# Products with w_o between the last heads of both mixers, and weight splits taken from POOL

## Chip, cores and metric

One core of one Trainium2 chip. The metric is device time of one execution in microseconds (us), the median of the runs shown.

## What is computed

The reference, cut to what matters here (x is 512 x 1024, two layers, all in fp32):

```python
for i in range(DEPTH):                      # 0: mixer A, 1: mixer B
    h = rms_norm(x, g_mix_pre[i])
    proj = h @ w_in[i]                      # q: 12 heads of 64, k and v: 3 heads, qm: 4 heads
    ...
    tok = mixer_a(...) if kind == 0 else mixer_b(...)
    mo = memory_attention(qm, km, vm)       # 4 heads on 256 memory rows
    o = jnp.concatenate([tok, mo], axis=-1) @ w_o[i]
    x = x + rms_norm(o, g_mix_post[i])
    h = rms_norm(x, g_ffn_pre[i])
    gu = h @ w_gate_up[i]
    f = (jax.nn.silu(gu[..., :D_FF]) * gu[..., D_FF:]) @ w_down[i]
    x = x + rms_norm(f, g_ffn_post[i])
```

Mixer A attends to a band of 128 tokens to either side with a sink logit per head; mixer B attends to all 512 tokens, with norms on q and k.

## The kernel before

Every fp32 operand of a large product is split into two parts, a high one (`hi`) and the rest (`lo`). A product is then three matmuls (`mm3`, lines 220 to 222 in the trace). `split` makes the parts: `hi` by ACT (line 230) or, if bit 2 of its last argument is set, by POOL (line 228); `lo` by DVE (line 234) or, with bit 1, by POOL (line 232). `unit` fetches a piece of a weight matrix of 128 x 1024 (or 768) by a DMA on SP's queue into one of three buffers and splits it, in halves of 512 columns where it is placed among the heads; four pairs of split units exist at a time.

The token rows lie in four row tiles of 128 (t = 0 to 3). A mixer runs in one order for PE that the kernel writes out: pieces of work are put at a place x, counted in heads, with `put(x, f)`, sorted and then issued. The places come from the table `PACE`, one entry per mixer, as do the engines for splits (`kw` for w_kv, `mw` for the memory weights, `qw` for w_q, `owm` for w_o, `tw` for the heads' outputs). The order of the other engines is made by a scheduler that follows the dependences.

At a mixer's start come the transposes of the normed rows (hT), the products with w_kv (`kv_pieces`), w_q (`q_pieces`) and the memory weights (`mem_pieces`). Then 12 token heads and 4 memory heads: scores (lines 511 and 512, memory scores 545 and 546), exponentials on ACT (528, 550), normalising of p on POOL (566), transposes of p on PE (576), splits of them (`th`, `tl`), the value product (590, 591) and the sum into `tok` on DVE (599).

`heads_out` places the work on w_o among the last heads: four units of the first 512 output columns, the splits of `tok` into `th` (`part(k)`, k = 0 to 7, one for each pair of heads), and the products of k = 0 to 5 for the row tiles 0 and 1, six matmuls at a time. `mix_out` follows the heads: it finishes the first 512 columns, squares them (ACT) and multiplies them by the gain (DVE), then does the second 512 columns row tile by row tile, with a norm and the residual. `ffn_out` is the end of the feed-forward part; for each row tile `join` adds, squares and multiplies, `post_norm` adds the residual and gives the normed row h for the next layer.

PSUM's eight banks are called acc (2), s (3), pv (1) and t (2). Scores take s, value products pv, transposes of p and of the rows t, transposes of q for c > 0 acc. `bank` hands acc, acc, s, s, s, pv out in turn for the products with w_o.

```python
for k in range(KD):
    put(xs[k], lambda k=k: part(k))
for k in range(NH // 2):
    put(max(x0 + k * dx, xs[k] + 0.001), lambda k=k: prod(k))
```

Of the kernel before, what the change touches and what calls it, by code (L numbers as in the profile page):

```python
# [15 lines left out]
P = 128  # L16
# [15 lines left out]
BIG = 1e37  # L32
LOTS = ((0, 8), (8, 14), (14, 22))

PACE = [{'lag': 1.692, 'vlag': 0.479, 'jstep': 0.213, 'kstep': 0.375, 'klag': 0.742, 'qoff': [0.212, 0.126, 0.099], 'qlag': 1.02, 'late': 0.252, 'moff': -0.235, 'mdur': 0.562, 'mlag': 0.697, 'kw': [1, 0, 2, 0], 'mw': [2, 1, 1, 0], 'qw': [1, 0, 0, 1, 3, 3, 3, 3], 'hoff': 1.262, 'ow': 10.288, 'ox': 14.385, 'od': 0.906, 'hstep': 0.872, 'hlag': 1.742, 'hjstep': 0.135, 'hvlag': 0.751, 'owm': [3, 3, 3, 3, 3, 2, 0, 1], 'q0step': 0.27, 'q0off': -0.032, 'q0lag': 0.919, 'm0off': -0.078, 'm0dur': 0.002, 'm0lead': 1.887, 'mlead': 1.201, 'qlead': 0.921, 'q0lead': 1.555, 'qstep': 1.002, 'tw': [0, 0, 0, 1, 0, 1, 0, 0], 'h2off': 0}, {'lag': 1.824, 'vlag': 0.535, 'jstep': 0.218, 'kstep': 0.777, 'klag': 1.715, 'qoff': [-0.027, -0.162, -0.027], 'qlag': 1.189, 'late': 2.15, 'moff': -0.088, 'mdur': 0.384, 'mlag': 1.205, 'kw': [0, 0, 0, 0], 'mw': [2, 2, 0, 3], 'qw': [1, 0, 0, 0, 0, 3, 1, 1], 'hoff': 0, 'ow': 12.899, 'ox': 15.498, 'od': 0.513, 'hstep': 0.946, 'hlag': 1.847, 'hjstep': 0.295, 'hvlag': 0.568, 'owm': [3, 3, 3, 0, 3, 2, 0, 3], 'q0step': 0.718, 'q0off': -0.018, 'q0lag': 1.136, 'm0off': -1.059, 'm0dur': 0.171, 'm0lead': 2.465, 'mlead': 3.162, 'qlead': 1.895, 'q0lead': 1.42, 'qstep': 0.998, 'tw': [0, 1, 2, 3, 1, 0, 1, 0], 'h2off': 0.016}]
# [137 lines left out]
class Trunk:  # L173
# [139 lines left out]
    def bank(self):  # L313

        tag, bufs = (("acc", 2), ("acc", 2), ("s", 3), ("s", 3), ("s", 3), ("pv", 1))[self.nbank % 6]
        self.nbank += 1
        return self.ps.tile([P, 512], F32, tag=tag, name="ps", bufs=bufs)
# [15 lines left out]
    def mem_pieces(self, l, mk, put, x0, dx, lag, xw):  # L333

        w, ps = {}, []
        for u in range(4):
            self.unit(self.a["wm"][l, u], self.side(l, "mw", u), put=put, x=xw[u], dst=w, key=u)

        def prod(u, m):
            if u == 0:  # L340
                ps.append(self.ps.tile([P, 512], F32, tag="s", name="ps", bufs=3))
# [71 lines left out]
    def kv_pieces(self, l):  # L413
# [4 lines left out]
        w = self.wkv if l == 0 else [self.unit(self.a["wkv"][l, u], side=self.side(l, "kw", u)) for u in range(4)]  # L418
# [32 lines left out]
    def q_pieces(self, l, c, qTs, put, x0, lead):  # L451
# [29 lines left out]
        def stage(t, st):  # L481
            if c:
# [15 lines left out]
    def score(self, hd, i):  # L498
# [10 lines left out]
        s = self.ps.tile([P, 512], F32, tag="s", name="s", bufs=3)  # L509
# [23 lines left out]
    def score_mem(self, hd, i):  # L533
# [8 lines left out]
        s = self.ps.tile([P, 2, NMEM], F32, tag="s", name="s", bufs=3)  # L542
# [185 lines left out]
    def heads_out(self, l, put, xw, xs, x0, dx):  # L728
# [3 lines left out]
        for u in range(4):  # L732
            self.unit(self.a["wo"][l, 0, u], self.side(l, "owm", u), put=put, x=xw + u / 4, dst=self.wo, key=u)
# [8 lines left out]
        def prod(k):  # L742
            if k == 0:
                self.po.extend(self.bank() for _ in range(2))
            for t in range(2):
                self.prod(self.po[t], self.heads, KD, k, t, self.wo[k // 2])

        for k in range(KD):
            put(xs[k], lambda k=k: part(k))
        for k in range(NH // 2):  # L750
            put(max(x0 + k * dx, xs[k] + 0.001), lambda k=k: prod(k))
# [4 lines left out]
    def mix_out(self, l, forms, resid, dst):  # L756
# [57 lines left out]
    def tagged(self, tag):  # L814
        return self.ps.tile([P, 512], F32, tag=tag, name="ps", bufs={"acc": 2, "s": 3, "pv": 1, "t": 2}[tag])

    def ffn_out(self, get, w, fs, o, head, gpost, gpre, resid, dst, rs):
# [26 lines left out]
        for t in range(NT):  # L844
# [237 lines left out]
    def run(self):  # L1082
        tc, nc, a = self.tc, self.nc, self.a
        with ExitStack() as top:
# [5 lines left out]
            self.ps, self.nbank = self.psum(top, "ps"), 0  # L1090
# [84 lines left out]
```

## Time and profile before

| | us |
|---|---|
| median of 3 runs (1162.67 to 1164.7) | 1163.73 |
| profiled execution | 1161.5 |
| its span on the core | 1159.7 |
| PE busy | 1106.9 |
| DVE busy | 840.9 |
| ACT busy | 644.7 |
| POOL busy | 264.6 |

Times within the trace count from the start of the span. Mixer A's heads end near 183, mixer B's start lies at 570 to 640 and its heads end near 767; the feed-forward parts lie behind each mixer. A row of a timeline gives start, busy time, engine, line, operation and tiles, and in brackets how long the engine stood idle before it and what released it. Matmuls are pipelined: a row's own time is longer than the step from one matmul to the next.

### The profile page before, as it was taken

The page shows a single profiled execution, that of the slowest core. Times are in us where ns is not written, and L with a number is a line of the kernel's source. Part 1 is how long each engine was busy: PE and PEld are TensorE (multiplying, and loading weights), DVE is VectorE, ACT ScalarE, POOL GpSimd, SP SyncE. Part 2 cuts the span into 40 slices and gives each one's busy share as a digit, 9 for nine tenths or more (in the row PEclk, how much of TensorE's full clock was granted, in tenths as well). Part 3 has the DMA queues.
Part 4 walks back from the last instruction along what each step waited for, and adds up shares of the span by engine and source line. Part 5 has one row for each costly group of instructions (what it writes and reads, how often), then busy time and mean ns, then how long its engine had stood idle before and what let it go on. Part 6 is the DMA issues. An engine that isn't in the chain of part 4 may idle for free.

```text
span 1159.7 us, 19436 instructions
## 1 busy us (share of the span) xinstructions
PE 1106.9 (95%) x7448; PEld 1016.6 (88%) x7448; DVE 840.9 (73%) x1432; ACT 644.7 (56%) x1308; POOL 264.6 (23%) x394
## 2 busy tenths in 40 slices
PE   5999989999999999999898999799999999999997
PEld 4989878899989989998788888577999899899985
DVE  5678884798637866885778998846997458658854
ACT  5568783665425534653436888845665246436531
POOL 6445573200000000000454764433000000000001
PEclk9999999999999999999999999999999999999999
DMA  7521124533422342225523110234234323413243
GB/s 269 189 74 37 37 74 134 189 114 109 154 65 73 110 145 73 97 87 191 174 93 106 37 37 2 69 116 150 68 115 140 107 73 110 142 41 110 92 163 109
DMA packets 34316, 124.06 MB, mean 107 GB/s; under 512 B 3872, under 2 KB 4000, under 8 KB 34096
## 3 DMA queue, kind: packets, MB, share of 16 engines
q1 hardware_dynamic: 33984, 122.24, 32.0%
q8 instruction: 58, 0.95, 0.3%
q0 software_dynamic: 240, 0.60, 0.2%
q14 instruction: 34, 0.28, 0.1%
HBM read 112.33 MB, written 10.49 MB: 106 GB/s over the span
## 4 chain that ended last, share of the span: by engine, by line
PE 78%; DVE 9%; ACT 5%; POOL 3%; issue 3%; DMA 1%; SPq 0%; POOLq 0%; DVEq 0%; ACTq 0%
PE ps L220 12%; PE ps L221 12%; PE ps L222 12%; PE ps L930 11%; PE ps L932 11%; PE ps L931 11%; PE tp L576 2%; PE o L591 1%; PE o L590 1%; PE s L511 1%; DVE tl L234 1%; PE s L512 1%; DMA raw<-in_wkv_dram 1%; ACT whi L230 1%; ACT p L528 1%
## 5 line engine op out<-in xcount | busy, mean ns | idle before, releaser
L230 ACT ACTIVATE whi<-raw 128x1024 fp32r<-128x1024 f32 (+2 forms) x177 | 150.6, 860 | 208.6 <-PE ps L222 104.2
L234 DVE TENSOR_TENSOR wlo<-raw,whi 128x1024 fp32r<-128x1024 f32 (+2 forms) x171 | 171.5, 1009 | 89.9 <-ACT whi L230 74.2
L930 PE MATMUL ps<-sf,whi 128*128 128x256 f32 x640 | 180.3, 282 | 0.1
L932 PE MATMUL ps<-sf,whi 128*128 128x256 f32 x640 | 180.2, 282 | 0.0
L931 PE MATMUL ps<-sf,wlo 128*128 128x256 f32 x640 | 179.8, 281 | 0.0
L254 POOL TENSOR_SCALAR e<-sso 128x1 f32<-128x1 f32 x8 | 3.4, 423 | 634.7 <-ACT junk L249 634.6
L220 PE MATMUL ps<-whi,f 128*128 128x512 f32 x352 | 137.3, 390 | 0.0
L222 PE MATMUL ps<-whi,f 128*128 128x512 f32 x352 | 137.0, 389 | 0.0
L221 PE MATMUL ps<-wlo,f 128*128 128x512 f32 x352 | 137.0, 389 | 0.0
L930 PE MATMUL ps<-a,whi 128*128 128x256 f32 x480 | 134.5, 280 | 0.0
L932 PE MATMUL ps<-a,whi 128*128 128x256 f32 x480 | 134.0, 279 | 0.0
L931 PE MATMUL ps<-a,wlo 128*128 128x256 f32 x480 | 133.9, 279 | 0.0
L930 PEld LDWEIGHTS ps<-sf,whi 128*128 128x128 f32 x640 | 121.2, 189 | 1.1 <-ACT p L936 0.6
L931 PEld LDWEIGHTS ps<-sf,wlo 128*128 128x128 f32 x640 | 120.9, 189 | 0.5
L932 PEld LDWEIGHTS ps<-sf,whi 128*128 128x128 f32 x640 | 121.1, 189 | 0.0
L220 PE MATMUL ps<-whi,hT 128*128 128x256 f32 (+1 forms) x320 | 101.6, 318 | 1.8 <-ACT kx L434 1.8
L221 PE MATMUL ps<-wlo,hT 128*128 128x256 f32 (+1 forms) x320 | 96.8, 303 | 4.6 <-DVE wlo L234 3.4
L222 PE MATMUL ps<-whi,hT 128*128 128x256 f32 (+1 forms) x320 | 96.4, 301 | 0.8 <-DVE hT L234 0.8
L566 POOL TENSOR_SCALAR p<-p,rd 128x256 f32<-128x256 f32 (+2 forms) x128 | 74.9, 603 | 76.2 <-DVE rd L563 23.0
L930 PEld LDWEIGHTS ps<-a,whi 128*128 128x128 f32 x480 | 90.3, 188 | 0.2
L931 PEld LDWEIGHTS ps<-a,wlo 128*128 128x128 f32 x480 | 90.2, 188 | 0.2
L932 PEld LDWEIGHTS ps<-a,whi 128*128 128x128 f32 x480 | 90.2, 188 | 0.0
(202 smaller groups left out, 2805.0 us busy)
## 6 DMA issues: line engine op xcount, KB each, us to landing
raw<-in_wgu_dram SPq DMA_DIRECT2D x48, 512.0 KB, 4.3
raw<-in_wd_dram SPq DMA_DIRECT2D x44, 512.0 KB, 4.3
rb<-in_wgu_dram SPq DMA_DIRECT2D x40, 512.0 KB, 3.6
raw<-in_wq_dram SPq DMA_DIRECT2D x16, 512.0 KB, 3.8
raw<-in_wo_dram SPq DMA_DIRECT2D x16, 512.0 KB, 3.5
xt<-x SPq DMA_DIRECT2D x12, 512.0 KB, 4.1
raw<-in_wm_dram SPq DMA_DIRECT2D x8, 512.0 KB, 4.0
x<-y SPq DMA_DIRECT2D x8, 512.0 KB, 2.9
```

The lines of the kernel that those rows point to most:

```text
L220: mm(out, lh, rh, start=first, stop=False)
L221: mm(out, lh, rl, start=False, stop=False)
L222: mm(out, ll, rh, start=False, stop=last)
L230: nc.scalar.activation(hi, src, AF.Copy)
L234: nc.vector.tensor_sub(lo, src, hi.bitcast(F32))
L511: nc.tensor.matmul(s[:, :n], qi, hd["ka"]()[:, k0 * P:k1 * P], start=True, stop=False)
L512: nc.tensor.matmul(s[:, :n], qi, hd["kb"]()[:, k0 * P:k1 * P], start=False, stop=True)
L566: self.pooled = nc.gpsimd.tensor_scalar(hd["p"][z][:, :n], hd["p"][z][:, :n], rd[:, z:z + 1], 1.0, op0=OP.mult, op1=OP.mult)
L576: nc.tensor.transpose(tp[:, z], hd["p"][i][:, jj * P:(jj + 1) * P], self.ident)
L930: mm(out, wh[:, s], rh, start=start and k == 0, stop=False, skip_group_check=True)
L931: mm(out, wl[:, s], rh, start=False, stop=False, skip_group_check=True)
L932: mm(out, wh[:, s], rl, start=False, stop=k == 3, skip_group_check=True)
```

## The change

The products with w_o for k = 0 to 5 are placed for three row tiles (`NFILL`), each by itself, every 0.3 head from head 11.4 (A) or 11.3 (B) on. The third row tile takes one of the three s banks while it is being summed; scores go round on the other two (`turns`, `held`). The transposes of q for the row tiles 2 and 3 of the memory heads take t banks. The w_o units, and the splits of `tok`, are all made by ACT and DVE. In mixer B's start the memory weights and the first half of w_q are split by ACT and DVE as well, and the four w_kv units are created in `ffn_out` ahead of the join of its last row tile.

```diff
+NFILL = 3
...
 PACE[0]:
-'hoff': 1.262, 'ow': 10.288, 'ox': 14.385, 'od': 0.906
+'hoff': 0, 'ow': [10.3, 10.8, 12.2, 13.2], 'ox': 11.4, 'od': 0.3
-'owm': [3, 3, 3, 3, 3, 2, 0, 1], 'tw': [0, 0, 0, 1, 0, 1, 0, 0]
+'owm': [0, 0, 0, 0, 0, 0, 0, 0], 'tw': [0, 0, 0, 0, 0, 0, 0, 0]
 PACE[1]:
-'mw': [2, 2, 0, 3], 'qw': [1, 0, 0, 0, 0, 3, 1, 1], 'ow': 12.899, 'ox': 15.498, 'od': 0.513
+'mw': [0, 0, 0, 0], 'qw': [0, 0, 0, 0, 0, 3, 1, 1], 'ow': [10.2, 10.7, 12.2, 13.2], 'ox': 11.3, 'od': 0.3
-'owm': [3, 3, 3, 0, 3, 2, 0, 3], 'tw': [0, 1, 2, 3, 1, 0, 1, 0]
+'owm': [0, 0, 0, 0, 0, 0, 0, 0], 'tw': [0, 0, 0, 0, 0, 0, 0, 0]
...
 kv_pieces:
-        w = self.wkv if l == 0 else [self.unit(self.a["wkv"][l, u], side=self.side(l, "kw", u)) for u in range(4)]
+        w = self.wkv
...
 q_pieces, stage:
-            if c:
+            if c and (c, t) not in ((3, 2), (3, 3)):
...
 score, score_mem:
-        s = self.ps.tile([P, 512], F32, tag="s", name="s", bufs=3)
+        s = self.tagged("s", "s")
...
 heads_out:
-        def prod(k):
-            if k == 0:
-                self.po.extend(self.bank() for _ in range(2))
-            for t in range(2):
-                self.prod(self.po[t], self.heads, KD, k, t, self.wo[k // 2])
+        def prod(k, t):
+            if t == len(self.po):
+                self.po.append(self.bank())
+                if t == 2:
+                    self.held = self.turns.pop()
+            self.prod(self.po[t], self.heads, KD, k, t, self.wo[k // 2])
...
-            put(xs[k], lambda k=k: part(k))
+            put(max(xs[k], x0 + (NFILL * k - 1.5) * dx) if k < NH // 2 else xs[k], lambda k=k: part(k))
         for k in range(NH // 2):
-            put(max(x0 + k * dx, xs[k] + 0.001), lambda k=k: prod(k))
+            for t in range(NFILL):
+                put(max(x0 + (NFILL * k + t) * dx, xs[k] + 0.001 * (t + 1)), lambda k=k, t=t: prod(k, t))
...
 mix_out:
-        po = self.po + [self.bank() for _ in range(2)]
+        po = self.po + [self.bank() for _ in range(NT - NFILL)]
+        self.turns.insert(0, self.held)
...
-                for t in range(0 if k >= NH // 2 else 2, NT):
+                for t in range(0 if k >= NH // 2 else NFILL, NT):
...
 tagged:
+        if tag == "s":
+            self.turns.append(self.turns.pop(0))
+            return self.ps.tile([P, 512], F32, tag=self.turns[-1], name=name, bufs=1)
...
 ffn_out:
+            if gn is not None and t == NT - 1:
+                self.wkv = [self.unit(self.a["wkv"][1, u]) for u in range(4)]
             join(ps, t, 1)
```

Lines of the changed kernel stand one higher for the splits and products (221 to 223 for `mm3`, 235 for DVE's `lo`).

PE in the last heads of mixer A (`o<-th,vs` is a value product, `s<-ka,qT` a score, `tp<-ident,p` a transpose of p, `ps<-whi,th` and `ps<-wlo,th` products with w_o). Before:

```order
L590 MATMUL o<-th,vs 128x384
L591 MATMUL o<-tl,vs 128x384
L511 MATMUL s<-ka,qT 128x384
L512 MATMUL s<-kb,qT 128x384
L590 MATMUL o<-th,vs 128x384
L591 MATMUL o<-tl,vs 128x384
L576 MATMUL tp<-ident,p 128x128 x2
L511 MATMUL s<-ka,qT 128x256
L512 MATMUL s<-kb,qT 128x256
```

With the change:

```order
L590 MATMUL o<-th,vs 128x384
L591 MATMUL o<-tl,vs 128x384
L221 MATMUL ps<-whi,th 128x512
L222 MATMUL ps<-wlo,th 128x512
L223 MATMUL ps<-whi,th 128x512
L511 MATMUL s<-ka,qT 128x384
L512 MATMUL s<-kb,qT 128x384
L590 MATMUL o<-th,vs 128x384
L591 MATMUL o<-tl,vs 128x384
L576 MATMUL tp<-ident,p 128x128 x2
L221 MATMUL ps<-whi,th 128x512
L222 MATMUL ps<-wlo,th 128x512
```

Three matmuls with w_o for one row tile stand between a value product and the next score while the last token head's scores are made; before, the first six stood behind a memory head, some 58 rows later.

POOL in the same mixer, between the normalising of one head and the next (`whi<-raw`, `wlo<-raw,whi` are the splits of w_o). Before:

```order
L566 TENSOR_SCALAR p<-p,rd 128x256
L228 TENSOR_SCALAR whi<-raw 128x512 x2
L232 TENSOR_TENSOR wlo<-raw,whi 128x512 x2
L228 TENSOR_SCALAR whi<-raw 128x512 x2
L232 TENSOR_TENSOR wlo<-raw,whi 128x512
L566 TENSOR_SCALAR p<-p,rd 128x256
L566 TENSOR_SCALAR p<-p,rd 128x384 x2
L566 TENSOR_SCALAR p<-p,rd 128x256
L232 TENSOR_TENSOR wlo<-raw,whi 128x512
```

With the change:

```order
L566 TENSOR_SCALAR p<-p,rd 128x256 x2
L566 TENSOR_SCALAR p<-p,rd 128x384 x2
L566 TENSOR_SCALAR p<-p,rd 128x256 x2
L566 TENSOR_SCALAR p<-p,rd 128x384 x2
L566 TENSOR_SCALAR p<-p,rd 128x256 x2
```

Four first halves and four second halves, of two w_o units, are gone from between the heads' normalising; the rest of POOL's row of heads stays as it was.

DVE where the feed-forward part of layer 0 passes into mixer B (`wlo<-raw,whi 128x768` is a w_kv unit, `o<-o,ps` the first operation of the join, `h<-o,gain` the normed row, `hT<-tp,hT` the split of its transposes). Before:

```order
L713 SCALAR_TENSOR_TENSOR o<-o,ro,xt 128x512 x2
L234 TENSOR_TENSOR wlo<-raw,whi 128x768
L287 TENSOR_TENSOR h<-o,gain 128x1024
L234 TENSOR_TENSOR wlo<-raw,whi 128x768
L827 TENSOR_TENSOR o<-o,ps 128x512
L234 TENSOR_TENSOR hT<-tp,hT 128x4x128 x2
L831 TENSOR_TENSOR o<-o,gain 128x512
L713 SCALAR_TENSOR_TENSOR o<-o,ro,xt 128x512 x2
L234 TENSOR_TENSOR wlo<-raw,whi 128x768
L287 TENSOR_TENSOR h<-o,gain 128x1024
L234 TENSOR_TENSOR wlo<-raw,whi 128x768
```

With the change:

```order
L713 SCALAR_TENSOR_TENSOR o<-o,ro,xt 128x512 x2
L235 TENSOR_TENSOR wlo<-raw,whi 128x768
L288 TENSOR_TENSOR h<-o,gain 128x1024
L235 TENSOR_TENSOR wlo<-raw,whi 128x768 x2
L235 TENSOR_TENSOR hT<-tp,hT 128x4x128 x2
L834 TENSOR_TENSOR o<-o,ps 128x512
L235 TENSOR_TENSOR wlo<-raw,whi 128x768
L838 TENSOR_TENSOR o<-o,gain 128x512
L713 SCALAR_TENSOR_TENSOR o<-o,ro,xt 128x512 x2
L288 TENSOR_TENSOR h<-o,gain 128x1024
```

The third unit's split moves from behind the last row tile's join and residual to a place ahead of them, the fourth from behind h to a place between two operations of the join.

## Rows read from the trace of the kernel before

**Rows 1.** The page, part 1, PE: busy us (share), instructions; then the weight loads.

```profile
PE 1106.9 (95%) x7448; PEld 1016.6 (88%) x7448; DVE 840.9 (73%) x1432; ACT 644.7 (56%) x1308; POOL 264.6 (23%) x394
```

**Rows 2.** Busy time by stage: stretch, length; busy us of PE, PEld, DVE, ACT, POOL; clock; DMA share.

```profile
112.00:148.00 36.00, 34.12 (x271) 32.88 (x270) 31.09 (x87) 29.80 (x87) 21.25 (x31) 1.00 0.10 30
148.00:184.00 36.00, 31.32 (x185) 26.60 (x184) 28.69 (x60) 28.84 (x80) 20.13 (x32) 0.95 0.28 89
184.00:204.00 20.00, 20.00 (x90) 16.57 (x89) 5.95 (x10) 5.53 (x14) 8.20 (x12) 1.00 0.47 158
...
684.00:720.00 36.00, 34.44 (x240) 30.75 (x239) 31.23 (x67) 29.66 (x68) 20.86 (x29) 1.00 0.10 30
720.00:768.00 48.00, 40.35 (x230) 32.57 (x228) 36.76 (x64) 36.07 (x88) 24.23 (x34) 0.96 0.20 67
```

**Rows 3.** Timeline of PE, last heads of mixer A: start, us, what [idle before <-releaser].

```profile
122.51 0.41 PE L576 MATMUL tp<-ident,p 128*128 128x128 f32 x2 [1.15 <-DVE qx L385]
...
150.81 0.52 PE L576 MATMUL tp<-ident,p 128*128 128x128 f32 x3 [2.30 <-DVE den L562]
```

**Rows 4.** Timeline of POOL, 114 to 128.

```profile
116.89 2.54 POOL L232 TENSOR_TENSOR wlo<-raw,whi 128x512 fp32r<-128x512 f32 x2
...
121.83 2.14 POOL L566 TENSOR_SCALAR p<-p,rd 128x256 f32<-128x256 f32 x4
```

**Rows 5.** Timelines of POOL and of DVE, 143 to 154.

```profile
146.82 2.96 POOL L232 TENSOR_TENSOR wlo<-raw,whi 128x512 fp32r<-128x512 f32 x2
...
146.84 1.82 DVE L234 TENSOR_TENSOR th<-tok,th 128x512 fp32r<-128x512 f32 x1
```

**Rows 6.** Instructions on tok, 140 to 200: ns min/median/max.

```profile
L230 ACT ACTIVATE th<-tok x8: 612/632/664, 144.7 to 182.8; 128x512 fp32r<-128x512 f32 x8
L234 DVE TENSOR_TENSOR th<-tok,th x6: 682/864/1823, 145.3 to 183.4; 128x512 fp32r<-128x512 f32 x6
```

**Rows 7.** Timeline of PE, 572 to 584, start of mixer B.

```profile
572.45 0.33 PE L222 MATMUL ps<-whi,hT 128*128 128x384 f32 x1
572.62 0.34 PE L220 MATMUL ps<-whi,hT 128*128 128x384 f32 x1
576.36 0.69 PE L221 MATMUL ps<-wlo,hT 128*128 128x384 f32 x1 [3.40 <-DVE wlo L234]
576.85 0.52 PE L222 MATMUL ps<-whi,hT 128*128 128x384 f32 x1
...
581.73 0.52 PE L222 MATMUL ps<-whi,hT 128*128 128x384 f32 x1
```

**Rows 8.** Timeline of DVE, 567 to 579.

```profile
575.35 0.95 DVE L234 TENSOR_TENSOR wlo<-raw,whi 128x768 fp32r<-128x768 f32 x1
```

**Rows 9.** Timelines of PE at 610 and of DVE at 607 and 584.

```profile
610.09 0.59 PE L375 MATMUL tp<-identr,k 128*128 128x128 f32 x3 [3.25 <-DVE kb L376]
...
607.21 1.48 DVE L404 TENSOR_TENSOR rt<-kx,gt 128x96 f32<-128x96 f32 x2
...
584.88 0.42 DVE L404 TENSOR_TENSOR rt<-kx,gt 128x96 f32<-128x96 f32 x2
```

**Rows 10.** Timelines of PE and POOL, last heads of mixer B.

```profile
693.82 0.47 PE L590 MATMUL o<-th,vs 128*128 128x512 f32 x1 [1.56 <-DVE tok L599]
...
689.78 2.90 POOL L232 TENSOR_TENSOR wlo<-raw,whi 128x512 fp32r<-128x512 f32 x2
...
729.65 1.08 PE L576 MATMUL tp<-ident,p 128*128 128x128 f32 x4 [2.62 <-DVE rd L563]
```

**Rows 11.** Timelines of PE and of ACT, memory scores of mixer A.

```profile
156.40 0.36 PE L545 MATMUL s<-kma,qT 128*128 128x256 f32 x1
...
167.53 0.36 PE L545 MATMUL s<-kma,qT 128*128 128x256 f32 x1
...
171.68 0.36 PE L545 MATMUL s<-kma,qT 128*128 128x256 f32 x1
...
170.66 0.49 ACT L550 ACTIVATE p<-s,nm 128x256 f32<-128x256 f32 x1
```

More of the change, by code (lines that the diff above doesn't have):

```diff
@@ new lines @@
+PACE = [{'lag': 1.692, 'vlag': 0.479, 'jstep': 0.213, 'kstep': 0.375, 'klag': 0.742, 'qoff': [0.212, 0.126, 0.099], 'qlag': 1.02, 'late': 0.252, 'moff': -0.235, 'mdur': 0.562, 'mlag': 0.697, 'kw': [1, 0, 2, 0], 'mw': [2, 1, 1, 0], 'qw': [1, 0, 0, 1, 3, 3, 3, 3], 'hoff': 0, 'ow': [10.3, 10.8, 12.2, 13.2], 'ox': 11.4, 'od': 0.3, 'hstep': 0.872, 'hlag': 1.742, 'hjstep': 0.135, 'hvlag': 0.751, 'owm': [0, 0, 0, 0, 0, 0, 0, 0], 'q0step': 0.27, 'q0off': -0.032, 'q0lag': 0.919, 'm0off': -0.078, 'm0dur': 0.002, 'm0lead': 1.887, 'mlead': 1.201, 'qlead': 0.921, 'q0lead': 1.555, 'qstep': 1.002, 'tw': [0, 0, 0, 0, 0, 0, 0, 0], 'h2off': 0}, {'lag': 1.824, 'vlag': 0.535, 'jstep': 0.218, 'kstep': 0.777, 'klag': 1.715, 'qoff': [-0.027, -0.162, -0.027], 'qlag': 1.189, 'late': 2.15, 'moff': -0.088, 'mdur': 0.384, 'mlag': 1.205, 'kw': [0, 0, 0, 0], 'mw': [0, 0, 0, 0], 'qw': [0, 0, 0, 0, 0, 3, 1, 1], 'hoff': 0, 'ow': [10.2, 10.7, 12.2, 13.2], 'ox': 11.3, 'od': 0.3, 'hstep': 0.946, 'hlag': 1.847, 'hjstep': 0.295, 'hvlag': 0.568, 'owm': [0, 0, 0, 0, 0, 0, 0, 0], 'q0step': 0.718, 'q0off': -0.018, 'q0lag': 1.136, 'm0off': -1.059, 'm0dur': 0.171, 'm0lead': 2.465, 'mlead': 3.162, 'qlead': 1.895, 'q0lead': 1.42, 'qstep': 0.998, 'tw': [0, 0, 0, 0, 0, 0, 0, 0], 'h2off': 0.016}]
@@ L313, in bank @@
     def bank(self):
-        tag, bufs = (("acc", 2), ("acc", 2), ("s", 3), ("s", 3), ("s", 3), ("pv", 1))[self.nbank % 6]
         self.nbank += 1
-        return self.ps.tile([P, 512], F32, tag=tag, name="ps", bufs=bufs)
+        return self.tagged(("acc", "acc", "s", "s", "s", "pv")[(self.nbank - 1) % 6])
     def new_hT(self):
@@ L340, in prod @@
             if u == 0:
-                ps.append(self.ps.tile([P, 512], F32, tag="s", name="ps", bufs=3))
+                ps.append(self.tagged("s"))
             for k in (2 * u, 2 * u + 1):
@@ L541, in score_mem @@
         nm, den = hd["nm"], hd["den"]
-        s = self.ps.tile([P, 2, NMEM], F32, tag="s", name="s", bufs=3)
+        s = self.tagged("s", "s").rearrange("p (z n) -> p z n", z=2)
         for z in range(2):
@@ L732, in heads_out @@
         for u in range(4):
-            self.unit(self.a["wo"][l, 0, u], self.side(l, "owm", u), put=put, x=xw + u / 4, dst=self.wo, key=u)
+            self.unit(self.a["wo"][l, 0, u], self.side(l, "owm", u), put=put, x=xw[u], dst=self.wo, key=u)
         def part(k):
@@ L812, in down_prod, with tagged @@
             self.mm3(ps, get(0, k, t), get(1, k, t), wu[0][:, c], wu[1][:, c], k == 0, k == len(fs) - 1)
-    def tagged(self, tag):
-        return self.ps.tile([P, 512], F32, tag=tag, name="ps", bufs={"acc": 2, "s": 3, "pv": 1, "t": 2}[tag])
+    def tagged(self, tag, name="ps"):
+        if tag == "s":
+            self.turns.append(self.turns.pop(0))
+            return self.ps.tile([P, 512], F32, tag=self.turns[-1], name=name, bufs=1)
+        return self.ps.tile([P, 512], F32, tag=tag, name=name, bufs={"acc": 2, "pv": 1, "t": 2}[tag])
     def ffn_out(self, get, w, fs, o, head, gpost, gpre, resid, dst, rs):
@@ L1089, in run @@
             self.whl = self.pool(top, "whl")
-            self.ps, self.nbank = self.psum(top, "ps"), 0
+            self.ps, self.nbank, self.turns = self.psum(top, "ps"), 0, ["s0", "s1", "s2"]
             dram = top.enter_context(tc.tile_pool(name="dram", bufs=1, space=bass.MemoryType.DRAM))
```

1 line of the change is left out of this document (removed).

## Prediction

> **What bounds the kernel now.** I read the page first: PE is busy for 1106.9 of 1159.7 us [rows 1], so over the whole span only some 53 us of idle PE can be won, besides time that PE spends at its lower clock. The table by stage comes next [rows 2]. It shows where the idle time sits that this change can touch: in the last heads of mixer A (112 to 184) PE idles 1.88 + 4.68 us, in those of mixer B (684 to 768) 1.56 + 7.65 us, while directly behind the heads, at 184, PE is busy without a gap: 90 matmuls of 512 columns in 20.00 us, 0.222 us each. So work that stands behind the heads costs its full length, and there are holes ahead of it into which it could go. Third, the PE timeline names what ends the holes, and the timelines of POOL and DVE say why the releaser was late.
>
> In A, PE waits 1.15 and 2.30 us ahead of transposes of p [rows 3]. The row names DVE for the first, but what is transposed is p, and POOL does splits of w_o (2.54 us for two) ahead of normalising it from 121.83 on [rows 4]. For the second DVE is late: its split of th takes 1.82 us while POOL splits a weight at the same time [rows 5]; the same split takes 0.68 us at best [rows 6]. At the start of mixer B PE waits 3.40 us for the third unit of w_kv, and then runs at the lower level of its clock: 16 matmuls of 384 columns start between 576.85 and 581.73, 0.325 us apart, where they stood 0.17 apart before the wait [rows 7]. The releaser is DVE's split of that unit, started at 575.35 [rows 8]. PE also waits 3.25 us for kb: a pair of rope products takes DVE 1.48 us, while POOL splits memory weights, against 0.42 for a pair of the same line elsewhere [rows 9]. In B's last heads the waits are 1.56 us, with POOL at splits of w_o for 2.90 us until just before, and 2.62 us [rows 10].
>
> **The change part by part.** *Products moved, A.* PE's number of products is the same. Per mixer 30 matmuls of 512 columns leave the gapless stretch behind the heads (of 144 between the last value product and the next transposes 114 stay): 30 x 0.222 = 6.7 us off the path there. They come back between the heads. What that costs is bounded by 0 (all of them fall into holes) and 6.7 (each pushes the head behind it). A's last heads have 6.56 us of idle PE [rows 2], about as much as is put in; the products stand singly, three matmuls (0.67 us) at a time, where they stood in sixes. But PE will not find all of its holes: I let 1.7 us of the 6.7 come back, and take **-5.0**.
>
> *Products moved, B.* The same 6.7 us; the holes are larger (9.2 us) and the waits longer. I let 1.2 come back: **-5.5**.
>
> *Splits taken from POOL, last heads.* In A the first four w_o units go over whole: 8 first halves of 0.63 us to ACT and 8 second halves of 0.68 to DVE, and 2 second halves of th to DVE [rows 6]: ACT +5.0, DVE +6.8 us. Between 112 and 184 ACT then has 58.6 + 5.0 = 63.6 and DVE 59.8 + 6.8 = 66.6 of 72 us [rows 2], less what DVE gets back when POOL no longer splits beside it (1.14 us at the one split of rows 5). In B three whole units and some of th go over: 8 first halves for ACT (+5.0) and 10 second halves for DVE (+6.8), which makes 70.7 and 74.8 of 84. Both engines are close to full but not beyond it, so the heads can keep their length. The wait of 1.15 us behind POOL's splits [rows 3, 4] should go, and that of 1.56 [rows 10]; next late are ACT and DVE themselves. Bounds 0 and the whole wait each; I take **-1.0** and **-1.2**. The longer waits of 2.30 and 2.62 us are not booked again: they are the holes that the products fill. The splits of the second half's units, behind the heads, meet a DVE that is busy for 5.95 of 20 us there [rows 2] and cost nothing.
>
> Against this part stands a rule of the Trainium skill, page "Perfetto Trace Analysis", section "Optimizing Scalar/DVE Operations": when DVE is saturated, handing work to Scalar or even GPSIMD may make sense; the change does the reverse, at a DVE that is 77 to 87% busy in these stretches [rows 2]. The same paragraph adds that GPSIMD and DVE share a read port, so that offloading between the two might not help. By the first half of the rule the tails would give nothing and the sum would be that of the second rival below; the split that took 1.82 us beside POOL's own stands for the second half.
>
> *Start of B.* The splits of w_kv come earlier: DVE's third stands ahead of the join of the last row tile, its fourth still behind the first operation of that join. PE's third unit should be ready about when PE needs it; for the fourth a wait of 1 us or so is left. Bounds: 0 (the fourth split becomes the whole wait) and 3.40 + 16 x (0.325 - 0.17), which is 5.9 us. I take **-4.0**, near the upper end, because the first of the two splits that are late leaves the queue behind the join altogether. POOL's splits for memory weights and for one half of w_q go to ACT (6 first halves) and DVE (2 + 2 second halves, +2.7 us): the rope pair of 1.48 us should come near 0.42 again, but DVE has more to do. Bounds 0 and the 3.25 us wait; the row's own excess is 1.06 us and there are more operations of the chain like it: **-2.0**.
>
> *Third bank.* The third row tile takes one of the three score banks, so scores go round on two. And the second half of the output's columns begins in the bank of that third tile, which must first be squared by ACT and multiplied by DVE. PE waits there, bounded by 0 and by two operations of the length of rows 6 (1.3 us), 0.5 in each mixer: **+1.0**. Two transposes of q per mixer move to the banks of the other transposes; their cover is that these banks turn over with each head, and I cost them at nothing (without cover, up to an ACT copy of 0.63 us each). The loads of w_o are asked for earlier in B; the DMA share in that stretch is 0.10 [rows 2], so they land in time at no cost.
>
> *Sum.* -1.0 - 5.0 - 4.0 - 2.0 - 1.2 - 5.5 + 1.0 = **-17.7 us**. The profiled execution took 1161.5 us, which makes 1143.8; it is 2.2 us under the median of the runs, 1163.7, so against that I forecast 1146.0.
>
> **The rivals.** *The whole of it.* Every bound at its good end: 1.15 + 6.7 + 2.30 + 5.9 + 3.25 + 1.56 + 6.7 + 2.62 - 1.0 = 29 us, 1135. For it: the half clock goes with its waits. Against: ACT and DVE are at 85 to 90% and more afterwards.
>
> *ACT and DVE set the pace of the last heads.* With 66.6 of 72 us DVE has little slack, and heads go through ACT, DVE, POOL and PE one after the other; then each product only displaces, all 13.4 us come back, and what is left is 1.0 + 6.0 + 1.2 - 1.0 = 7.2 us: 1156.5, or 1153 to 1160 with the neighbours. The first half of the rule from the Trainium skill's "Perfetto Trace Analysis" would lead here too. For it: PE's two longest waits in these heads are for DVE [rows 3, 10]. Against: part of DVE's time is its slowing beside POOL [rows 5, 6].
>
> *The start of B doesn't do what it says.* The fourth w_kv split is still behind the join, and PE may wait there for as long as it did for the third. Then 4.0 us are missing: 1150.
>
> *Slower: two score banks.* A score bank is held from the first matmul of a pair of memory scores to the end of its last exponential, 167.53 to 171.15, 3.62 us in A [rows 11]. The eight pairs start between 156.40 and 171.68, one every 2.18 us [rows 11]; on three banks a hold of 6.5 us is free, on two 4.36 us. Above that every pair costs half the excess, 4 us per mixer for each us of hold. The sum of 17.7 us is eaten where the hold reaches 6.6 us; at 8 us, the hold with seven more ACT operations of 0.63 us in front, it is 2 x 4 x 3.64 = 29 us, 1175. For it: the splits added to ACT stand in that queue. Against: the margin of 0.74 us swallows one such split for each pair, and there are about as many splits as pairs.
>
> **How the numbers follow.** Forecast with its own range of 1138 to 1152: 0.50. The B start that keeps its wait (about 1150): 0.10. ACT and DVE as the pace (1153 to 1160): 0.20. The whole of it (1130 to 1138): 0.11. No difference that a measurement of this kernel can tell, within 0.2% or 2.3 us: 0.03. Slower, by two banks: 0.06. So faster 0.91, same 0.03, slower 0.06. The range of 1134 to 1158 leaves out some 0.04 below, and above it slower, same and the upper part of the pace case, 0.13.
>
> **What would show it.** Right: no weight splits on POOL in the last heads of either mixer; idle PE in those heads under 4 us for each mixer, and the gapless stretch behind them shorter by 6.7 us; the wait in front of the third w_kv unit gone and one of about 1 us in front of the fourth; th splits near 0.68 us on DVE. A wait of about 0.5 us in the middle of each w_o product. Wrong: the stretch from the same head to the last value product longer by 5 us or more (the pace rival), or waits on score matmuls for exponentials (two banks), or a wait of 3 us in front of the fourth w_kv unit.

## The result

The changed kernel takes 1146.66 us (median of 4 runs, 1145.04 to 1147.33) against 1163.2 before; the ratio is 0.9854 with an interval of 0.9837 to 0.9871. The forecast was 1146.0, 0.7 us away. The profiled execution has a span of 1143.3 us, 16.4 less than before.

The page's first part after the change:

```profile
PE 1098.8 (96%) x7448; PEld 1008.1 (88%) x7448; DVE 842.6 (74%) x1464; ACT 659.7 (58%) x1340; POOL 201.1 (18%) x330
```

POOL's time fell by 63.5 us, ACT's rose by 15.0, DVE's by only 1.7 although it makes 32 splits more (x1464 for x1432), of 0.68 us each: beside POOL it had been slower. PE's own busy time fell by 8.1 us with the same 7448 matmuls; its mean granted clock rose from 0.988 to 0.996, so this is, as far as the means show, time at its lower level that is gone.

Where the time went is read from the starts of the same matmuls in both PE timelines, as differences: the first score of a mixer, the first score of the last token head, the last value matmul, the first transpose behind the heads, the first product with w_kv. One execution each, in us:

| stretch | before | after | difference | forecast |
|---|---|---|---|---|
| up to the first score of A | 70.2 | 69.6 | -0.6 | 0 |
| A, first score to head 11 | 77.8 | 75.9 | -2.0 | -1.0 |
| A, head 11 to the last value matmul | 32.9 | 36.6 | +3.7 | +1.7 |
| A, behind the heads | 32.9 | 27.3 | -5.6 | -6.2 |
| B, first w_kv product to first score | 58.9 | 51.3 | -7.6 | -6.0 |
| B, first score to head 8 | 69.8 | 68.1 | -1.7 | -1.2 |
| B, head 8 to the last value matmul | 66.5 | 69.5 | +3.0 | +1.2 |
| B, behind the heads | 33.8 | 28.1 | -5.7 | -6.2 |

The two feed-forward parts between these stretches are as long as before (356.6 and 352.3). So the sum came out, and several of its terms did not: the last heads took back 3.7 and 3.0 us of what was pulled out from behind them, where I had let 1.7 and 1.2 come back; the start of B gave more.

The table of busy time by stage, columns as in [rows 2], for the last heads of A and the stretch behind them, the start of B, and the same for B's last heads:

```profile
145.50:182.10 36.60, 33.25 (x201) 27.74 (x200) 28.72 (x61) 29.57 (x82) 12.65 (x24) 1.00 0.19 58
182.10:201.60 19.50, 18.58 (x82) 15.03 (x81) 10.67 (x17) 9.11 (x21) 1.58 (x6) 1.00 0.59 216
...
566.00:586.00 20.00, 18.35 (x114) 17.63 (x113) 16.15 (x33) 10.69 (x26) 7.48 (x13) 1.00 0.38 127
...
711.00:755.00 44.00, 39.09 (x223) 31.24 (x221) 33.03 (x61) 32.70 (x81) 13.55 (x24) 1.00 0.14 49
755.00:775.00 20.00, 19.12 (x82) 15.11 (x82) 10.80 (x17) 9.33 (x21) 1.56 (x6) 1.00 0.57 211
```

The clock is 1.00 in all of these, where it was 0.95 and 0.96 in the last heads before [rows 2]. Of the last heads' idle PE 3.35 us remain in A (36.60 - 33.25) and 4.91 in B. The waits that remain, on the PE timeline:

```profile
148.16 0.51 PE L487 MATMUL tp<-identr,q 128*128 128x128 f32 x4 [1.49 <-DVE tl L235]
...
155.54 0.54 PE L487 MATMUL tp<-identr,q 128*128 128x128 f32 x4 [0.92 <-DVE tl L235]
...
192.94 0.50 PE L221 MATMUL ps<-whi,th 128*128 128x512 f32 x1 [0.92 <-DVE y L777]
...
570.37 0.44 PE L222 MATMUL ps<-wlo,hT 128*128 128x384 f32 x1 [0.76 <-DVE wlo L235]
...
599.37 0.42 PE L375 MATMUL tp<-identr,k 128*128 128x128 f32 x3 [1.33 <-DVE kb L376]
...
714.83 0.51 PE L487 MATMUL tp<-identr,q 128*128 128x128 f32 x4 [2.21 <-DVE tl L235]
...
766.10 0.50 PE L221 MATMUL ps<-whi,th 128*128 128x512 f32 x1 [0.88 <-DVE y L777]
```

The waits of [rows 3], 1.15 and 2.30 us, are gone; in A's last heads stand 1.49 and 0.92 us for DVE's splits of p instead. In B a wait of 2.21 us for such a split stands about where the 2.62 us of [rows 10] stood. In front of the fourth w_kv unit PE waits 0.76 us (3.40 in front of the third before, [rows 7]), for kb 1.33 us (3.25, [rows 9]). New are 0.92 and 0.88 us in the middle of the products with w_o, for the bank of the third row tile, whose last reader is DVE's product y, and 0.88 us at 577.42, among the products with w_kv, for an operation of ACT. So the sign of idle PE under 4 us in the last heads came true in A and not in B. The th splits of [rows 6], up to 1.82 us, are even:

```profile
L235 DVE TENSOR_TENSOR th<-tok,th x8: 679/688/806, 142.8 to 184.6; 128x512 fp32r<-128x512 f32 x8
```

### The profile page after: what moved, and what is told of

Same layout as the page of the kernel before. It is cut to its first block, busy times and chain, and to the rows that moved or that the text cites. A ratio compares the mean times of both kernels' runs of the same rounds, so it can differ in the third digit from the quotient of the medians.

```text
span 1143.3 us, 19459 instructions
## 1 busy us (share of the span) xinstructions
PE 1098.8 (96%) x7448; PEld 1008.1 (88%) x7448; DVE 842.6 (74%) x1464; ACT 659.7 (58%) x1340; POOL 201.1 (18%) x330
## 4 chain that ended last, share of the span: by engine, by line
PE 77%; DVE 9%; ACT 7%; issue 3%; POOL 3%; DMA 1%; SPq 0%; POOLq 0%; DVEq 0%; ACTq 0%
PE ps L939 12%; PE ps L941 11%; PE ps L221 11%; PE ps L940 11%; PE ps L222 11%; PE ps L223 11%; PE tp L576 2%; PE o L590 1%; PE o L591 1%; DVE tl L235 1%; ACT whi L231 1%; PE s L511 1%; PE s L512 1%; ACT p L528 1%; DVE wlo L235 1%
## 5 line engine op out<-in xcount | busy, mean ns | idle before, releaser
L231 ACT ACTIVATE whi<-raw 128x1024 fp32r<-128x1024 f32 (+2 forms) x207 | 168.0, 826 | 191.9 <-PE ps L941 95.3
L235 DVE TENSOR_TENSOR wlo<-raw,whi 128x1024 fp32r<-128x1024 f32 (+2 forms) x197 | 185.6, 953 | 75.9 <-ACT whi L231 74.8
L221 PE MATMUL ps<-whi,hT 128*128 128x256 f32 (+1 forms) x320 | 100.0, 313 | 2.7 <-ACT kx L434 2.7
L223 PE MATMUL ps<-whi,hT 128*128 128x256 f32 (+1 forms) x320 | 94.7, 296 | 0.8 <-DVE hT L235 0.8
```

What stands on the lines that cost most here:

```text
L221: mm(out, lh, rh, start=first, stop=False)
L223: mm(out, ll, rh, start=False, stop=last)
L231: nc.scalar.activation(hi, src, AF.Copy)
L235: nc.vector.tensor_sub(lo, src, hi.bitcast(F32))
```

## The experiments

The times below are medians of 4 to 6 runs; each stands beside its own runs of the kernel before (1163.4 to 1164.6 us, by group of experiments). A difference of medians of two groups is therefore uncertain by about 1 us; ratios allow for it.

### The two places apart

The first leaves out the part at B's start (w_kv made in `kv_pieces` again, `mw` and `qw` of B as before), the second has only that part, in the kernel before.

```diff
 e1_tails_only, against the change:
-            if gn is not None and t == NT - 1:
-                self.wkv = [self.unit(self.a["wkv"][1, u]) for u in range(4)]
...
-'mw': [0, 0, 0, 0], 'qw': [0, 0, 0, 0, 0, 3, 1, 1]
+'mw': [2, 2, 0, 3], 'qw': [1, 0, 0, 0, 0, 3, 1, 1]
```

> The change without its part at the start of mixer B: w_kv is made and split where it was before, and POOL splits memory weights and half of w_q there again. If the parts are independent, as the sum of the prediction takes them, the 7.65 us that the start of B gave come back, and nothing else moves: 1146.7 + 7.7 = 1154.3 us. If instead the head of B's attention depended on how the start went (the rival: what comes early at the start is lost at the next wait), less than 3 us come back: under 1150.

> The kernel before with only the part at the start of mixer B (w_kv early, no memory-weight and first w_q splits on POOL there). Independent parts: 1163.2 - 7.7 = 1155.5 us, with the first score of B about 7.65 us earlier and the heads as long as before. If what comes early is lost at the next wait: over 1160.

Measured: 1156.2 us without the start (ratio 0.9937, 0.9919 to 0.9955), 1153.5 us with the start alone (0.9913, 0.9893 to 0.9932). The start is worth 9.5 us in the one comparison and 9.9 in the other; the stretch from the first w_kv product to the first score is 59.0 us in the first and 51.2 in the second, 7.7 apart. Where the rest lies is not shown: without the start B's heads are 2.2 us longer than in the change, but with the start alone they are 0.9 longer than before. Both times are about 2 us off those expected, to either side. The parts are about independent, and the start is more than half of the whole gain.

### The start of B in two

```diff
 e6_wkv_back, against the change:
-            if gn is not None and t == NT - 1:
-                self.wkv = [self.unit(self.a["wkv"][1, u]) for u in range(4)]
...
-        w = self.wkv
+        w = self.wkv if l == 0 else [self.unit(self.a["wkv"][l, u], side=self.side(l, "kw", u)) for u in range(4)]
```

> The change with the w_kv units created where they were before, in the mixer itself; POOL still splits no memory weights and no first half of w_q at B's start. By the prediction's terms the 4.0 us booked for w_kv come back and the 2.0 for kb stay: 1146.7 + 4.0 = 1150.7. By the trace the first score of B came 7.65 us earlier relative to the start of w_kv's products; if most of that is POOL's part, the time is under 1149, if it is w_kv's, 1151 to 1154. The wait in front of the third unit should be back at 3 us or more.

Measured: 1152.2 us (0.9897, 0.9878 to 0.9916). The stretch is 55.4 us: between 59.0 with neither and 51.3 with both. So the splits taken from POOL give 3.6 us there, and w_kv early 4.1 on top of them, against 2.0 and 4.0 in the sum (by the medians w_kv is 5.5, with what follows in the heads). The other order, w_kv early with the splits on POOL, was not run. PE's timeline of this kernel shows the wait back, and the one for kb as short as in the change:

```profile
571.93 0.45 PE L222 MATMUL ps<-wlo,hT 128*128 128x384 f32 x1 [3.40 <-DVE wlo L235]
...
603.27 0.42 PE L375 MATMUL tp<-identr,k 128*128 128x128 f32 x3 [1.36 <-DVE kb L376]
```

### Products and splits apart

The third run has the products where they were, with all splits on ACT and DVE; the fourth has the products where the change puts them, with the w_o and th splits on POOL again. With the change and the run of the start alone they make a square, all four with the new start of B.

```diff
 e3_products_back: heads_out, mix_out and the banks of q's transposes of the kernel before; in PACE, places as before
-'hoff': 0, 'ow': [10.3, 10.8, 12.2, 13.2], 'ox': 11.4, 'od': 0.3
+'hoff': 1.262, 'ow': 10.288, 'ox': 14.385, 'od': 0.906
...
 e4_pool_back: in PACE, splits as before
-'owm': [0, 0, 0, 0, 0, 0, 0, 0], 'tw': [0, 0, 0, 0, 0, 0, 0, 0]
+'owm': [3, 3, 3, 3, 3, 2, 0, 1], 'tw': [0, 0, 0, 1, 0, 1, 0, 0]
...
```

> The change with its products in the old places (two row tiles, in sixes, from the first memory heads on, three score banks, w_o loads and splits at their old places), but all splits on ACT and DVE. Theory (products fill holes, and the splits that left POOL make the heads shorter): the waits behind POOL stay away (2.6 us in A, 1.7 in B), and the last heads get shorter since less stands in them, but 6.7 us per mixer stand behind the heads again: 1149 to 1153 us. Rival (ACT and DVE set the pace of the last heads, products only displace): the heads' length does not depend on the products, so the time is that of the change plus up to 13: 1156 to 1160. Second rival (the products give nothing at all in the last heads, all of it is POOL): within 2 us of the change, under 1149.

> The change with the splits of w_o and of the heads' outputs on POOL as before, in the new places. Theory (POOL's splits stand ahead of the normalising of p and slow DVE): the waits behind POOL come back, 2.6 us in A and 1.7 in B, and some 1 to 2 us per mixer in the last heads: 1151 to 1155 us. Rival (ACT and DVE set the pace, since 5 and 6.8 us per mixer leave them): faster than the change, 1140 to 1146.

| us (ratio) | splits on POOL as before | splits on ACT and DVE |
|---|---|---|
| products behind the heads as before | 1153.5 (0.9913) | 1147.5 (0.9859) |
| products between the heads | 1157.4 (0.9946) | 1146.7 (0.9854) |

This overturns the sum's reasons for the heads. With the splits on POOL in the new places the time is above the 1151 to 1155 us that were expected. Without the products' new places the change would be at 1147.5: they give 0.8 us, which the intervals (0.9841 to 0.9877 and 0.9837 to 0.9871) do not separate from nothing. With POOL at the splits the new places cost 3.9 us. And taking the splits from POOL gives 6.0 us in the old places and 10.7 in the new ones, where I had booked 2.2.

Why the products give so little is in the table by stage. The last heads of A in two pieces, for the kernel before, for the run with the products back, and for the change:

```profile
148.00:165.00 17.00, 12.36 (x76) 10.55 (x74) 14.42 (x36) 13.94 (x41) 12.38 (x18) 0.90 0.19 63
165.00:180.90 15.90, 15.85 (x95) 13.47 (x96) 13.02 (x23) 13.68 (x39) 7.76 (x15) 1.00 0.30 86
```

```profile
144.70:161.00 16.30, 11.87 (x79) 9.36 (x77) 15.24 (x38) 15.83 (x46) 4.90 (x10) 1.00 0.20 65
161.00:176.90 15.90, 15.81 (x96) 13.17 (x94) 13.10 (x24) 13.54 (x37) 6.72 (x15) 1.00 0.27 89
```

```profile
145.50:157.00 11.50, 8.88 (x58) 7.38 (x57) 10.75 (x29) 11.40 (x32) 3.54 (x7) 1.00 0.32 92
157.00:182.10 25.10, 24.37 (x145) 20.36 (x144) 17.97 (x33) 18.17 (x52) 9.11 (x18) 1.00 0.13 43
```

The holes lie in the first piece, which in the first two kernels ends at about the same work and in the change, cut at 157.0, earlier in the order. There PE idles 4.64 us before (17.00 - 12.36), 4.43 with the splits gone and 2.62 in the change. So the splits' going took away the long wait of A and the lower clock (0.90 to 1.00), but hardly any of the idle time: shorter waits for DVE came instead, the longest 1.06 us. ACT, at 82% before, is at 97% and 99% once it makes the splits (15.83 of 16.30, 11.40 of 11.50). In the second piece PE is busy for 15.85 of 15.90 us before the change already.

How much of the products the holes took up is read at one and the same matmul behind the first piece, for the three kernels in the same order:

```profile
165.50 0.34 PE L591 MATMUL o<-tl,vs 128*128 128x384 f32 x1
...
161.16 0.33 PE L591 MATMUL o<-tl,vs 128*128 128x384 f32 x1
...
163.79 0.34 PE L591 MATMUL o<-tl,vs 128*128 128x384 f32 x1
```

From the first score of head 11 (148.03, 144.68 and 145.46) it is 17.5 us to this matmul before, 16.5 with the products back and 18.3 in the change, where seven of A's 18 products stand ahead of it. They are 4.7 us of work (7 x 0.67) and cost 1.8, so 2.9 us fell into holes. Behind it, up to the last value product, 11 products stand instead of 8: 2.0 us of work, which cost 2.6 (18.3 for 15.7). There PE has nothing to spare, and products push out what follows.

With the splits on POOL the first piece is worse still. The waits of the fourth run, and POOL and DVE ahead of them:

```profile
151.50 0.52 PE L576 MATMUL tp<-ident,p 128*128 128x128 f32 x3 [2.30 <-DVE den L562]
153.18 0.72 PE L487 MATMUL tp<-identr,q 128*128 128x128 f32 x4 [1.16 <-DVE tl L235]
...
163.28 0.51 PE L487 MATMUL tp<-identr,q 128*128 128x128 f32 x4 [1.06 <-DVE rd L563]
...
147.51 2.96 POOL L233 TENSOR_TENSOR wlo<-raw,whi 128x512 fp32r<-128x512 f32 x2
150.44 1.64 POOL L229 TENSOR_SCALAR whi<-raw 128x512 fp32r<-128x512 f32 x2
...
153.30 2.22 POOL L566 TENSOR_SCALAR p<-p,rd 128x256 f32<-128x256 f32 x4
...
147.53 1.82 DVE L235 TENSOR_TENSOR th<-tok,th 128x512 fp32r<-128x512 f32 x1
```

```profile
148.70:164.00 15.30, 10.77 (x56) 9.39 (x55) 10.63 (x27) 10.11 (x30) 9.99 (x12) 0.78 0.23 69
```

Splits stand in POOL's queue from 145.91 to 153.30 without a break; DVE's split of th takes 1.82 us beside them; PE waits 2.30 us, as before [rows 3], and then twice more, and its clock is 0.78 on the average of the stretch. The wait of 2.30 us is DVE's: its three splits of th between 146.05 and 151.02 take 1.01, 1.82 and 1.35 us beside POOL's, where 0.68 is the shortest, which makes 2.1 us more, and PE goes on 0.15 after the split of p behind them is done. At the lower level the products just put there take longer too: three start 0.42 us apart at 156, 0.23 apart at 161. None of these waits is for a split that POOL makes.

### Two row tiles, early

```diff
 e7_two_tiles, against the change:
-NFILL = 3
+NFILL = 2
...
-        self.turns.insert(0, self.held)
```

> The change with NFILL = 2: products for two row tiles only, singly and early, three score banks again, 18 matmuls per mixer fewer between the heads than in the change. Theory after the runs so far (once POOL's splits are gone, what is put between the heads mostly displaces, about 4.4 of 6.7 us): within 1.5 us of the change, 1145.5 to 1148. Rival (two score banks cost the last heads something that the third tile's products pay back): faster than the change by over 2 us.

Measured: 1157.95 us (0.9947, 0.9933 to 0.996), 11 us slower than the change: neither expectation. From the same table with 36 instead of 54 matmuls per mixer between the heads, A's last heads are longer, not shorter (38.9 us), and 30.2 us stand behind them. The products come at the same distance of 0.3 head, and so for k = 4 and 5 earlier than in the change; PE now waits for th, and at the end of the memory heads, where no product is left, for tok:

```profile
170.40 0.50 PE L221 MATMUL ps<-whi,th 128*128 128x512 f32 x1 [1.36 <-ACT th L231]
...
171.66 0.50 PE L223 MATMUL ps<-whi,th 128*128 128x512 f32 x1 [0.52 <-DVE th L235]
...
179.43 0.50 PE L590 MATMUL o<-th,vm 128*128 128x512 f32 x1 [1.52 <-DVE tok L599]
...
182.68 0.50 PE L590 MATMUL o<-th,vm 128*128 128x512 f32 x1 [1.19 <-DVE tok L599]
```

So the memory heads do leave gaps where no product stands, at their end above all; the 24 matmuls of the old places, late and in sixes, cover those as well as the 54 of the change.

### What POOL's work costs by itself

In four runs ACT and DVE make the splits as in the change, and POOL does something without use on the first four (A) and three (B) units of w_o: behind the other engines' splits, or as soon as a unit has landed; and either two operations of the splits' kind, which read, or three fills, which do not. (The fills that go as soon as the unit has landed stand behind an operation on one column, which waits for the unit.)

```diff
 e8_pool_reads (e9_pool_fills: three fills of r instead), against the change, in unit:
             self.split(hi[:, c0:c1], lo[:, c0:c1], raw[:, c0:c1], side)
+            if extra:
+                g, r = nc.gpsimd, raw[:, c0:c1]
+                g.tensor_scalar(r, r, 1.0, 1.0, op0=OP.mult, op1=OP.mult)
+                g.tensor_tensor(r, r, r, op=OP.subtract)
...
 e10_pool_lump_reads (e11_pool_lump_fills: the first on one column, then three fills of d), ahead of the split, into a tile of its own:
+                g.tensor_scalar(d, r, 1.0, 1.0, op0=OP.mult, op1=OP.mult)
+                g.tensor_tensor(d, r, d, op=OP.subtract)
```

> The change, but POOL does two operations without use on the raw weights behind each split of the first four (A) and three (B) w_o units, of the same form and size as the splits that it did before; ACT and DVE still do all the splits that count, so no product waits for POOL's. If it is POOL's queue ahead of the normalising of p, and DVE slowed beside it, that cost the time, most of what the run with POOL's splits lost (10.7 us) is lost here: 1152 to 1158 us. If it was that products waited for splits which POOL makes slowly, none: under 1149.

> As the run before, but with three fills of constants per half unit on POOL, which read nothing. If DVE's slowing beside POOL is what costs (its splits read two tiles while POOL reads), the time is that of the change, 1146 to 1149 us, and DVE's splits of th stay near 0.68 us. If POOL's queue ahead of the normalising costs, the loss is as large as with the reading operations, in proportion to POOL's added time in both.

> The change, with POOL doing operations without use, of the splits' form and size, on each half of the first four (A) and three (B) w_o units as soon as it is loaded, so that they stand in lumps of several ahead of the normalising of p, as the splits did; nobody waits for their results. Theory now: POOL's added work costs where it stands in a lump in front of a p that PE needs, and beside DVE's own splits: 1149 to 1154 us. Rival: it costs only where its results are needed (splits that are late), and then this run is at 1147, as the run with the useless operations behind the other engines' splits was.

> As the run before, but the useless operations are fills that read nothing (three of 0.53 us for each half unit, 1.6 us against about 1.7). If the lump in POOL's queue costs, the same time as the run before within 1.5 us. If DVE's slowing by POOL's reading costs, the time of the change, 1146 to 1148, while the run before is slower.

Measured: behind the splits 1147.0 us (0.9867, 0.9848 to 0.9886) with reading operations and 1147.65 (0.9859, 0.9844 to 0.9873) with fills, both like the change; as soon as the unit has landed 1155.15 us (0.9923, 0.9904 to 0.9942) with reading operations and 1150.85 (0.9883, 0.9862 to 0.9903) with fills. The reading run of the first pair fell short of my expectation: there POOL's work is released half by half by DVE's own splits, and in its rows at 144 to 151 and 672 to 688 it stands in pairs, with gaps or the normalising between them. In the second pair nobody waits for its results either, yet 8.5 and 4.2 us are lost (8.0 and 3.4 by the ratios; the interval with fills just overlaps that of the change). The fills lie between their two expectations, all of the loss and none. POOL and PE in the run with reading operations:

```profile
627.77 0.62 POOL L200 TENSOR_SCALAR spare<-raw 128x512 f32<-128x512 f32 x1 [2.15 <-DMA raw<-in_wo_dram]
628.47 1.30 POOL L201 TENSOR_TENSOR spare<-raw,spare 128x512 f32<-128x512 f32 x1
629.86 0.62 POOL L200 TENSOR_SCALAR spare<-raw 128x512 f32<-128x512 f32 x1
630.57 1.41 POOL L201 TENSOR_TENSOR spare<-raw,spare 128x512 f32<-128x512 f32 x1
632.06 0.25 POOL L249 TENSOR_SCALAR r<-ss 128x4 f32<-128x4 f32 x1
632.40 1.03 POOL L250 TENSOR_TENSOR r<-r,mhalf 128x4 f32<-128x4 f32 x1
633.41 2.87 POOL L570 TENSOR_SCALAR p<-p,rd 128x512 f32<-128x512 f32 x4
...
634.17 0.33 PE L580 MATMUL tp<-ident,p 128*128 128x128 f32 x1 [0.29 <-POOL p L570]
635.00 0.33 PE L580 MATMUL tp<-ident,p 128*128 128x128 f32 x1 [0.50 <-POOL p L570]
635.67 0.33 PE L580 MATMUL tp<-ident,p 128*128 128x128 f32 x1 [0.34 <-POOL p L570]
636.33 0.47 PE L580 MATMUL tp<-ident,p 128*128 128x128 f32 x1 [0.34 <-POOL p L570]
```

Four useless operations, 4.2 us from start to end, stand ahead of a row norm r that was due and of the normalising of p; each transpose of p then waits for POOL, 0.29 to 0.50 us. From the first score of B to head 8 this kernel takes 72.9 us, the change 68.1, the one with fills 69.6. These operations do not stand where the splits stood before, since they go as soon as the data is there; they show what a row of POOL's work ahead of its small operations costs, not the exact price at the old places, which is the square's. At the old places the long waits were DVE's, as was shown above for the run with the splits back on POOL. Why reading costs 4.3 us more than filling was not traced to single instructions, except that the clock falls to 0.91 between 635 and 655 in the one and stays at 1.00 in the other.

### The bank of the third row tile

```diff
 e5_bank_last, against the change; e12_both also sets B's 'qw' to zeros:
-        self.turns.insert(0, self.held)
+        self.turns.append(self.held)
```

> The change, but the third row tile's score bank is handed back as the last in turn instead of the first, so that the second half's first row tile takes another score bank, long free. If the wait in the middle of each w_o product (0.92 and 0.88 us on the trace) is for that bank's readers, both waits go: 1146.7 - 1.8 = 1144.9 us. Rival: PE meets the next wait (w_o units of the second half, which ACT and DVE split just then) and the time stays at 1146.7.

> The change with the third tile's score bank handed back last, and no w_q splits on POOL in mixer B either. The bank gave 3.0 us (1143.6). A wait of 0.69 us and a row norm behind POOL's splits of w_q remain at 656 in the kernel before; without them, if POOL's lumps cost there too, 1141.5 to 1143; if ACT and DVE are what is late in these heads, the same as with the bank alone, 1143.6, or up to 2 us slower. The feed-forward part of the second layer took 350.3 us with the bank handed back last and 352.3 in every other run: if that hangs on the order of the banks it is 350.3 here too.

Measured: 1143.6 us (0.9829, 0.9815 to 0.9843) for the bank alone, 1145.5 (0.9835, 0.9817 to 0.9854) for both. The two waits of 0.9 us are gone from both traces: behind the heads stand 26.1 us in A and 27.0 in B instead of 27.3 and 28.1. The remaining splits of w_q on POOL in B cost nothing that shows. The kernel with the bank handed back last has the lowest median of all; its interval touches that of the change, and 2 us of its profiled run have another cause, told below, so that the 2.4 us on the trace are the better evidence. So the waits ate most of what the products' new places gave: with the bank handed back last these would be worth some 3 us (an estimate, 0.8 from the square and 2.4 from here).

## Why the prediction was right, and where it was not

*The total.* 1146.0 against 1146.7 is partly luck, since the errors of the terms met: 4.9 us too much for the last heads and what stands behind them, 1.6 too little at B's start, 1.5 too little for the two stretches of heads ahead of them, and 0.6 before A's first score, where nothing was changed.

*Products moved.* This is the step that failed. I put idle PE of 6.56 us beside 6.7 us of products for A and took them to fit. Nearly all of the 4.68 us of it in A's last heads lies at 148 to 165, while 11 of the 18 products stand behind that, where PE was busy for 15.85 of 15.90 us. Each term of -5.0 and -5.5 should have been about -1, or -2 without the waits for the third bank, which the sum has as a term of its own: from the run with the products back to the change, A's last heads and the stretch behind them give 65.1 - 64.0 = 1.1 us, B's 98.5 - 97.6 = 1.0 (from head 8 on), and the medians 0.8 altogether. The second rival, ACT and DVE as the pace, with its 13.4 us that come back, came nearer: all but 2.1 of them did by these stretches, the 1.8 us of waits for the bank among them. ACT is nearly full, at 97 to 99%, only in the first piece, and the waits that PE has there are named for DVE; behind that it is PE that is full.

*Splits taken from POOL.* Booked with 2.2 us for two waits, measured as 6.0 in the old places and 10.7 in the new. I had left the waits of 2.30 and 2.62 us to the products as holes to fill. From the run of the start alone to the run with the products back, both without the new places, the stretches give 1.8 us in A up to head 11, 0.7 in A's last heads, 1.0 in B up to head 8 and 3.3 in B's last heads (the first is hardly more than single profiles differ there). The last is, with the splits on POOL and without:

```profile
689.10:757.10 68.00, 60.50 (x365) 50.49 (x364) 53.34 (x100) 52.91 (x126) 32.27 (x46) 0.95 0.11 37
```

```profile
685.70:750.40 64.70, 58.49 (x366) 48.22 (x365) 54.69 (x106) 54.77 (x132) 22.22 (x36) 1.00 0.15 47
```

Idle PE falls from 7.50 to 6.21 us, and its busy time by 2.0 with practically the same matmuls, as its clock rises from 0.95 to 1.00. So a good part of what the splits cost was not the wait but PE at its lower level behind it, for which the sum had nothing in these heads. In A the holes stayed, in smaller waits. This is also why the rival's price of 1156.5 did not come out.

Why the waits were there I had half right. The wait of 1.15 us in A I put to POOL's normalising, against the row. By the timelines of the kernel before it is DVE's, like the one of 2.30: a product of the rope takes 1.33 us beside a split on POOL (most of its form take 0.16 to 0.20), the split of p follows it and ends at 122.36, and PE goes on at 122.51.

```profile
120.57 1.27 POOL L232 TENSOR_TENSOR wlo<-raw,whi 128x512 fp32r<-128x512 f32 x1
...
120.56 1.33 DVE L384 TENSOR_TENSOR rt<-qx,ropet 128x32 f32<-128x32 f32 x1
```

*Start of B.* Right in kind, and 7.6 for 6.0: w_kv 4.1 (booked 4.0; the wait in front of the fourth unit came out at 0.76 us for 1), the splits 3.6 (booked 2.0), in the one order that was run. The rival that the start does not do what it says is refuted: the wait of 3.40 us is gone in the change, and returns when w_kv goes back.

*Third bank.* The wait in the middle of the w_o product was 0.92 and 0.88 us where 0.5 was taken, within the bound of 1.3, and it goes with the order of the banks, which gives 2.4 us on the trace. Two score banks cost nothing that shows: no wait of a score matmul for an exponential stands among the named waits of the last heads. By this that rival is refuted in this kernel.

*The rule.* The first half of the rule from the Trainium skill, "Perfetto Trace Analysis", section "Optimizing Scalar/DVE Operations", to offload a full DVE to GPSIMD, would have kept the splits on POOL. Here that costs 6 to 11 us. DVE's busy time rose by only 1.7 us with the work it took over, which speaks for the caution in the same paragraph.

## What to carry to other kernels

Set idle time beside added work stretch by stretch, not for a stage as a whole: holes ahead of the place where work is put do not take it up. Work given to one engine can slow another: here DVE's operations beside POOL's splits, which PE then waited for; compare the length of one and the same operation beside such work and away from it. An engine that makes small operations on which everyone waits should not have long independent ones queued ahead of them either, even if nobody needs their results soon; look for it in that engine's timeline just before the small operation. And when a wait is filled with other work, first ask what made it, since the cause may be part of the same change; and look whether its going leaves smaller waits in its place.

## What was not expected of the hardware

POOL slows some of DVE's operations and not others. In the kernel before, beside the same splits of POOL that stretched DVE's split of th to 1.82 us [rows 5], DVE's splits of transposed p, which read one tile from PSUM, kept their length (0.52 to 0.56 us for all 24 of this form, before and in the change alike):

```profile
151.81 0.54 DVE L234 TENSOR_TENSOR tl<-tp,th 128x384 fp32r<-128x384 f32 x1
...
151.36 1.28 POOL L232 TENSOR_TENSOR wlo<-raw,whi 128x512 fp32r<-128x512 f32 x1
```

The Trainium skill, page "SBUF — State Buffer", section "Who interferes with whom", says that a DVE instruction with two inputs in SBUF contends with a GpSimd instruction that reads SBUF, and that one with at most one such input, outside the 2-port modes, does not. Both rows agree with it: 0.54 us beside a POOL split of 1.28 us, against 1.82 for the split with two such inputs.

The step of PE at a granted clock of 1.00 is not always the same. In the profiled run with the bank handed back last, 256-column matmuls of the second feed-forward part start 0.113 us apart from 818 to 866 and 0.118 in every other profile; that part is 350.3 us long in this one profile and 352.3 in all others, the run with the same order of banks and no w_q splits among them. So it is not the banks, and its cause stays open; 2 of the 2.1 us by which this profile ends ahead of the change's are this, which is why the waits and not the ends were compared above.

Kernels that are the same up to head 11 of A differ there by up to 1.5 us between single profiles (74.4 to 75.9 us with all splits of w_o off POOL). Differences of that size in one stretch of one profile were not read as effects by themselves.
